# The last layer norm: only the mean goes through TensorE's offset product, and the offset row is added by VectorE and GpSimd

## The chip, the cores and the metric

One core of a Trainium2 chip runs the whole kernel. It has five engines that run their own instruction streams and wait for each other by semaphores: TensorE (PE: matrix products into PSUM), VectorE (DVE), ScalarE (ACT), GpSimd (POOL) and SyncE (SP), which here only issues transfers. The metric is device time in microseconds (us): the median of several runs. The profiled execution is one further run, with its own time and its own span from the first to the last instruction.

## The reference: what is computed

Two layers over 256 rows of 2048 columns. Each layer projects the rows, mixes them in three groups of heads, gates, projects back (`out`), adds the residual and normalises:

```python
def layer_norm(x, g, b):
    mu = jnp.mean(xf, axis=-1, keepdims=True)
    var = jnp.mean(jnp.square(xf - mu), axis=-1, keepdims=True)
    y = (xf - mu) * lax.rsqrt(var + LN_EPS) * g + b
...
    out = y @ w_out
    return layer_norm(DEEPNORM_ALPHA * x + out, ln_g, ln_b)
```

The change concerns the norm of the second, last layer alone. With `rstd` for the reciprocal root, the result in each row is `(x - mu) * rstd * g + b`.

## The kernel before

All products are float32 made of three products of split operands, `hi*hi + lo*hi + hi*lo`, accumulated in PSUM over 16 slices of 128. The weights come in by SP's queue, are split by ScalarE and VectorE (`parts`, L126 to L129) and multiplied by the helper `mm` (L102). TensorE works through the groups of columns one after the other.

The 2048 columns of the output projection are four groups of 512 (`columns(n)`, n = 0 to 3), and the 256 rows are two halves (t = 0 and 1). `res` holds residual plus output. Groups 0 to 2 are finished first; `add_residual` adds them to `res`, takes their statistics, and for t = 1 VectorE multiplies them by the gain `g` at once (L1016). The last group (3) is made for t = 0 first, then for t = 1, and the latter ends with its columns 256 to 511 in a bank of their own (`rest`), so that most of the statistics are taken while TensorE still works.

`norm_last` (L704) is that end. For t = 0 everything is done by VectorE while TensorE makes the products of t = 1. For t = 1 the end of the kernel hangs on it, and it goes in two ways:

- Group 3, in two halves of 256 columns, by VectorE: `centred` (L720) computes `(r - mean) * g`, `result` (L750) computes `r * rstd + b` and stores.
- Groups 0 to 2, which hold `x * g` already, by TensorE and then one scaling. The product of the identity and `res` (L767) puts `x * g` into a PSUM bank, exact, in float32. Then `offsets` (L741) adds a product of 8 rows to it: `nparts`, the transposed small table `nt` with the two parts of `-mean` and of the standard deviation `std` for every row of t = 1, times `rows`, the parts of `g` and `b`. The bank then holds `(x - mean) * g + std * b`, and a multiplication by `rstd` out of PSUM (L782 on VectorE, L784 on ScalarE) gives the result, since `std * rstd` is 1.

`scales` (L722) makes `mvt` (mean and variance), `rstd` by a root on ScalarE and a correction step on VectorE, and for t = 1 the table `nt` (mean at L729 and L730, deviation at L736 to L738). Its argument `meanwhile` is work put between the root's start and its use. The table is turned by TensorE (L773) and copied out of PSUM by ScalarE (L774).

TensorE, SP and GpSimd run in the order of the program. VectorE and ScalarE are ordered by a planner that simulates the time, except in the block of `norm_last` from L753 on, where they too keep the program's order. `store` (L744) issues a transfer from SP's queue, or, for the last one (group 2), from ScalarE's. A transfer at the head of a queue that waits for its data holds those behind it. GpSimd does nothing in this tail.

Of the kernel before, what the change touches and what calls it, by code (L numbers as in the profile page):

```python
# [8 lines left out]
F32 = mybir.dt.float32  # L9
# [3 lines left out]
AF = mybir.ActivationFunctionType  # L13
ALU = mybir.AluOpType
# [4 lines left out]
P = 128  # L19
# [17 lines left out]
def hybrid_trunk_kernel(  # L37
# [7 lines left out]
    pe, dve, act, pool, sp = nc.tensor, nc.vector, nc.scalar, nc.gpsimd, nc.sync  # L45
# [51 lines left out]
    def nm(s):  # L97
        uid[0] += 1
        return f"{s}_{uid[0]}"

    def mm(o, l, r, start, stop):
        pe.matmul(o, l, r, start=start, stop=stop, skip_group_check=True)  # L102

    def bank():
        return psa.tile([P, 512], F32, name=nm("bk"), tag="bk")
# [4 lines left out]
    def small(shape, tag, bufs=1):  # L110
        return sm.tile(shape, F32, name=nm(tag), tag=tag, bufs=bufs)

    ident = cst.tile([P, P], F32, name="ident")
# [533 lines left out]
    def columns(n):  # L647
        return slice(n * 512, (n + 1) * 512)
# [7 lines left out]
    def add_residual(n, t, acc, stats, halves=2):  # L656

        r = res[:, t, columns(n)]
        dve.scalar_tensor_tensor(r, r, ALPHA, acc, op0=ALU.mult, op1=ALU.add)  # L659
        for i in range(halves):  # L660
            dve.bn_stats(stats[:, t, 2 * n + i], r[:, i * 256:(i + 1) * 256])
# [42 lines left out]
    def norm_last(accs, rest, stats, gb, rows, more):  # L704

        n = WO_N - 1
        mvt, rstd = [], []  # L710
        nparts = hd.tile([P, P], F32R, name="nparts", tag="qe")
        nt = sm.tile([P, 2, 4], F32R, name="nt1", tag="nt1")
        std = small([P, 1], "std")
        for t in range(2):
            mvt.append(small([P, 2], f"mvt{t}"))
            rstd.append(small([P, 1], f"rstd{t}"))

        def centred(i, t, c0=0, c1=512):
            r = res[:, t, i * 512 + c0:i * 512 + c1]
            dve.scalar_tensor_tensor(r, r, mvt[t][:, 0:1], gb[i][0][:, c0:c1], op0=ALU.subtract, op1=ALU.mult)  # L720

        def scales(t, meanwhile):  # L722
            dve.bn_aggr(mvt[t], stats[:, t])  # L723
            u, v = small([P, 1], f"rs_u{t}"), small([P, 1], f"rs_v{t}")
            act.activation(u, mvt[t][:, 1:2], AF.Sqrt, bias=eps[:, 0:1])
            dve.tensor_scalar(v, mvt[t][:, 1:2], LN_EPS, -0.5, op0=ALU.add, op1=ALU.mult)
            if t == 1:
                mean = mvt[t][:, 0:1].to_broadcast([P, 2])
                dve.tensor_scalar(nt[:, 0, 0:4:2], mean, -1.0, None, op0=ALU.mult)  # L729
                dve.scalar_tensor_tensor(nt[:, 1, 0:4:2], mean, -1.0, nt[:, 0, 0:4:2].bitcast(F32), op0=ALU.mult, op1=ALU.subtract)  # L730
            meanwhile()
            dve.reciprocal(rstd[t], u)
            dve.scalar_tensor_tensor(u, rstd[t], v, rstd[t], op0=ALU.mult, op1=ALU.mult)
            dve.scalar_tensor_tensor(rstd[t], u, 1.5, rstd[t], op0=ALU.add, op1=ALU.mult)
            if t == 1:
                dve.scalar_tensor_tensor(std, v, -2.0, rstd[t], op0=ALU.mult, op1=ALU.mult)  # L736
                dve.tensor_copy(nt[:, 0, 1:4:2], std.to_broadcast([P, 2]))
                dve.tensor_tensor(nt[:, 1, 1:4:2], std.to_broadcast([P, 2]), nt[:, 0, 1:4:2].bitcast(F32), op=ALU.subtract)  # L738

        def offsets(i, o):  # L740
            mm(o, nparts[:8], rows[i // 2][:8, i % 2 * 512:i % 2 * 512 + 512], False, True)  # L741

        def store(t, cs, queue=sp):
            queue.dma_start(out[t * P:(t + 1) * P, cs], res[:, t, cs])  # L744

        def result(i, t, c0=0, c1=512):

            cs = slice(i * 512 + c0, i * 512 + c1)
            r = res[:, t, cs]
            dve.scalar_tensor_tensor(r, r, rstd[t], gb[i][1][:, c0:c1], op0=ALU.mult, op1=ALU.add)  # L750
            store(t, cs)

        with tc.manual_schedule(engines={DVE, mybir.EngineType.Activation}):  # L753

            add_residual(n, 0, accs[0], stats)
            scales(0, lambda: centred(n, 0))
            result(n, 0)
            for i in range(n):
                centred(i, 0)
                result(i, 0)  # L760
            with tc.high_priority(AHEAD):
                more(0)
                add_residual(n, 1, accs[1], stats, 1)
                more(1)
                o = [psd.tile([P, 2, 512], F32, name=nm("acc"), tag="acc")[:, 0], bank(), bank()]
                for i in (1, 2, 0):
                    mm(o[i], ident, res[:, 1, columns(i)], True, False)  # L767
                r = res[:, 1, n * 512 + 256:n * 512 + 512]
                dve.tensor_tensor(r, r, rest, op=ALU.add)  # L769
                dve.bn_stats(stats[:, 1, 2 * n + 1], r)  # L770
                scales(1, lambda: centred(n, 1, 0, 256))
                pt = bank()
                pe.transpose(pt[:8, :P], nt.rearrange("p a b -> p (a b)").bitcast(F32), ident)  # L773
                act.copy(nparts[:8], pt[:8, :P])  # L774
                result(n, 1, 0, 256)
                centred(n, 1, 256, 512)
                result(n, 1, 256, 512)
                for i in (1, 0, 2):
                    offsets(i, o[i])
                    r = res[:, 1, columns(i)]  # L780
                    if i == 0:
                        dve.tensor_scalar(r, o[i], rstd[1], None, op0=ALU.mult)  # L782
                    else:
                        act.activation(r, o[i], AF.Copy, scale=rstd[1])  # L784
                    store(1, columns(i), act if i == 2 else sp)


    zeros = hd.tile([P, P], F32, name="zeros", tag="st")
# [5 lines left out]
    res = per.tile([P, 2, D], F32, name="res")  # L794
# [3 lines left out]
    for l in range(L):  # L798
# [90 lines left out]
        bias = {}  # L889
# [67 lines left out]
        last = l == L - 1  # L957
        stats = small([P, 2, 2 * WO_N, 6], "stats")
        gb = []
# [8 lines left out]
        for n in range(WO_N):  # L968
# [4 lines left out]
            if last and n == WO_N - 1:  # L973


                accs = [psd.tile([P, 2, 512], F32, name=nm("acc"), tag="acc")[:, 0], bank()]
                rest = bank()[:, :256]
                both = [operand()[2].rearrange("p (h k) n -> p h k n", h=2),
                        per.tile([P, 2, 2, 512], F32R, name=nm("late"), tag="asv")]
                homes = {pc: (x[:, 0], x[:, 1]) for pc, x in zip((2, 3), both)}  # L980
                for i, pc in enumerate((4, 5)):
                    homes[pc] = [per.tile([P, 2, 512], F32R, name=nm("late"), tag=f"yr{2 * i + k}") for k in range(2)]
                ws = [piece(src[pc], 512, 2, homes.get(pc)) for pc in range(8)]

                def products(o, t, kts, cs=slice(0, 512), first=0):
                    for kt in kts:
                        as_products(o, t, yq, [w[:, :, cs] for w in ws[kt // 2]], kt, kt % 2, first)

                products(accs[0], 0, range(16))

                def more(i):
                    if i == 0:
                        products(accs[1], 1, range(12))
                        products(accs[1][:, :256], 1, range(12, 16), slice(0, 256))
                    else:
                        products(rest, 1, range(12, 16), slice(256, 512), 12)

                norm_last(accs, rest, stats, gb, rows, more)
                break
# [4 lines left out]
            for m, pc in order:  # L1004
# [6 lines left out]
                if pc == 7:  # L1011
                    for t in range(2):
                        add_residual(m, t, accs[m][:, t], stats)
                    if last:
                        r = res[:, 1, columns(m)]
# [94 lines left out]
```

## Time and profile before

| | us |
|---|---|
| median of 3 runs | 900.3 |
| lowest and highest run | 900.08, 900.83 |
| the profiled execution, own time | 900.78 |
| its span | 899.0 |
| TensorE busy in the span | 891.3 |
| VectorE busy | 611.8 |
| ScalarE busy | 478.6 |
| GpSimd busy | 214.4 |

In the rows of the profile, a line of the timeline has start, duration, engine, source line, operation, what is written and read, and the count; in brackets the engine's idle time before it and what ended that wait. A name ending in q is an engine's queue, where transfers are issued. `bk` and `acc` are PSUM banks, `sc` are buffers that here hold `g` and `b` of a group, `gbrow` is a buffer of `rows`. A float32 product of 128x512 shows as two matrix instructions. A row of the transfers gives the count, the size of each and the time from issue to landing; a row by stretch gives the busy time of each engine with the count of its instructions.

### The profile page before, as it was taken

To read this page: it belongs to the slowest core of one execution; us is meant where nothing else is said; L and a number is where in the kernel's file an instruction comes from. 1 tells how busy PE (TensorE), PEld (TensorE's weight loads), DVE (VectorE), ACT (ScalarE), POOL (GpSimd) and SP (SyncE) were. 2 spreads that over 40 slices of the span, in tenths; PEclk is the share of its full clock that TensorE was granted. 3 is DMA by queue.
4 is the path that set the end of the run, shared out by engine and by line. 5 is a ranking of instruction groups with operands and counts; after the bars stand their busy time and mean duration, and the time that the engine had idled before them with its cause. 6 is when DMAs were issued, how large, how long until landed. Compare 5 with 4: busy or idle time off the path is not lost.

```text
span 899.0 us, 13806 instructions
## 1 busy us (share of the span) xinstructions
PE 891.3 (99%) x4687; PEld 746.6 (83%) x4687; DVE 611.8 (68%) x887; ACT 478.6 (53%) x686; POOL 214.4 (24%) x401
## 2 busy tenths in 40 slices
PE   9999999999999999999999999999999999999997
PEld 7888988888988888888888888888888888888885
DVE  6756568767477667665587777796565767676766
ACT  6644575555445566544476444854744457565440
POOL 0022103115315443410000221231061344433200
PEclk9999999999999999999999999999999999999999
DMA  8887779867989797975675859697479897979762
GB/s 309 310 260 226 231 235 268 262 207 220 275 254 241 236 271 238 316 236 188 227 241 184 233 164 286 195 292 213 150 224 296 244 270 221 287 217 289 218 183 94
DMA packets 164838, 213.74 MB, mean 238 GB/s; under 512 B 24752, under 2 KB 142896, under 8 KB 164768
## 3 DMA queue, kind: packets, MB, share of 16 engines
q1 hardware_dynamic: 148256, 173.29, 63.4%
q0 software_dynamic: 16224, 39.18, 15.2%
q8 instruction: 37, 0.61, 0.3%
q10 hardware_dynamic: 288, 0.39, 0.1%
q14 instruction: 33, 0.27, 0.1%
HBM read 193.20 MB, written 19.53 MB: 237 GB/s over the span
## 4 chain that ended last, share of the span: by engine, by line
PE 98%; DMA 1%; DVE 0%; ACT 0%; SPq 0%; issue 0%
PE acc L102 91%; PE bk L102 6%; DMA raw<-w 1%; PE bk L626 0%; ACT res L784 0%; SPq L179 0%; ACT wh L128 0%; DVE stats L770 0%; DVE res L769 0%; SPq L203 0%; SPq L201 0%; DVE res L720 0%; DVE mvt L723 0%; PE bk L773 0%; ACT nparts L774 0%
## 5 line engine op out<-in xcount | busy, mean ns | idle before, releaser
L102 PE MATMUL acc<-wh,x 128*128 128x512 f32 (+2 forms) x2516 | 749.4, 381 | 0.4 <-ACT wh L128 0.2
L102 PEld LDWEIGHTS acc<-wh,x 128*128 128x128 f32 x2516 | 460.7, 188 | 87.0 <-ACT wh L128 1.3
L129 DVE TENSOR_TENSOR wl<-raw,wh 128x1024 fp32r<-128x1024 f32 (+3 forms) x321 | 368.2, 1151 | 209.5 <-ACT wh L128 204.9
L128 ACT CAST wh<-raw 128x1024 fp32r<-128x1024 f32 (+3 forms) x321 | 318.7, 996 | 346.6 <-PE acc L102 212.8
L102 PE MATMUL acc<-wl,x 128*128 128x512 f32 (+2 forms) x1258 | 476.6, 379 | 0.0
L102 PEld LDWEIGHTS acc<-wl,x 128*128 128x128 f32 x1258 | 236.2, 188 | 45.6 <-DVE wl L129 1.1
L527 POOL DMA_DIRECT2D home<-sc x70 | 39.2, 560 | 458.1 <-DVE sc L525 442.6
L532 POOL DMA_DIRECT2D pT<-home x96 | 52.5, 553 | 28.5 <-DMA home<-sc 12.8
L532 POOL DMA_DIRECT2D qk<-home x64 | 34.9, 553 | 30.4 <-DMA home<-sc 28.5
L532 POOL DMA_DIRECT2D zT<-home x48 | 26.2, 552 | 21.8 <-DMA home<-sc 14.0
L525 DVE STREAM_TRANSPOSE sc<-sc 128x512 f32<-128x512 f32 (+1 forms) x38 | 24.9, 667 | 3.7 <-ACT sc L950 3.0
L532 POOL DMA_DIRECT2D yr<-home x48 | 26.3, 555 | 3.2 <-DMA home<-sc 3.2
L525 DVE STREAM_TRANSPOSE sc<-acc 128x512 f32<-128x512 f32 x28 | 18.3, 691 | 5.0 <-PE acc L102 4.8
L554 ACT ACTIVATE sc<-sc,mx 128x128 f32<-128x128 f32 (+1 forms) x32 | 14.4, 449 | 13.0 <-DVE mx L552 13.0
L547 DVE SCALAR_TENSOR_TENSOR sc<-bk,bias 128x384 f32<-128x384 f32 x16 | 8.6, 538 | 10.7 <-PE bk L102 10.7
L128 ACT CAST x<-sc 128x512 fp32r<-128x512 f32 x20 | 12.3, 617 | 5.0 <-DVE sc L508 3.8
L129 DVE TENSOR_TENSOR x<-sc,x 128x512 fp32r<-128x512 f32 x20 | 13.7, 685 | 1.4 <-ACT x L128 1.4
L102 PEld LDWEIGHTS bk<-pT,asv 128*128 128x128 f32 x64 | 11.8, 189 | 1.8
L102 PE MATMUL bk<-qk,qk 128*128 128x128 f32 (+1 forms) x64 | 13.1, 326 | 0.0
L102 PE MATMUL bk<-pT,asv 128*128 128x256 f32 (+1 forms) x64 | 13.0, 326 | 0.0
L659 DVE SCALAR_TENSOR_TENSOR res<-res,acc 128x512 f32<-128x512 f32 x15 | 9.7, 681 | 4.0 <-PE acc L102 4.0
L129 DVE TENSOR_TENSOR x<-raw,x 128x1024 fp32r<-128x1024 f32 x5 | 6.1, 1226 | 8.9 <-ACT x L128 8.8
(204 smaller groups left out, 506.4 us busy)
## 6 DMA issues: line engine op xcount, KB each, us to landing
raw<-w SPq DMA_DIRECT2D x387, 256.0 KB, 4.7
raw<-w SPq DMA_DIRECT2D x62, 512.0 KB, 4.9
home<-sc POOLq DMA_DIRECT2D x54, 256.0 KB, 4.3
raw<-w SPq DMA_DIRECT2D x32, 388.0 KB, 5.1
raw<-w SPq DMA_DIRECT2D x32, 264.0 KB, 3.3
qk<-home POOLq DMA_DIRECT2D x64, 64.0 KB, 5.2
raw<-w SPq DMA_DIRECT2D x32, 124.0 KB, 4.8
bias<-relw SPq DMA_DIRECT2D x16, 192.0 KB, 4.6
```

What stands on the lines that cost most here:

```text
L102: pe.matmul(o, l, r, start=start, stop=stop, skip_group_check=True)
L128: keep(act.copy(hi, src))
L129: keep(dve.tensor_tensor(lo, src, hi.bitcast(F32), op=ALU.subtract))
L525: dve.transpose(blocks.rearrange(order, j=32), src.rearrange("p (g b j) -> p g b j", b=4, j=32))
L527: pool.dma_start(homes[-1], blocks)
L532: pool.dma_start(dst[b * 32:(b + 1) * 32], home[:, b].rearrange("(a i) n -> i a n", a=4))
L547: dve.scalar_tensor_tensor(s, pb[:, :384], SCALE, bias[h], op0=ALU.mult, op1=ALU.add)
L554: act.activation(s[:, own[t]], s[:, own[t]], AF.Exp, bias=mx[:, t:t + 1], accum_out=zs[:, t:t + 1])
L659: dve.scalar_tensor_tensor(r, r, ALPHA, acc, op0=ALU.mult, op1=ALU.add)
```

## The change

The deviation no longer goes through the offset product. Its two places in `nt` are set to zero once, ahead of the block, and the three instructions that made it (L736 to L738) are gone; the bank then holds `(x - mean) * g`, and `b` is added behind the scaling by `rstd`.

- TensorE's order: the identity products of groups 2 and 0, the turning of `nt`, the offsets of groups 2 and 0, then the identity product and the offset of group 1. The turning and the copy `nparts` now stand inside `meanwhile`.
- Groups 0 and 1: VectorE computes `o * rstd + b` from PSUM in one instruction each.
- Group 2: ScalarE scales from PSUM, GpSimd adds `b` (512 columns).
- The second half of group 3 leaves VectorE: ScalarE computes `mean - r`, GpSimd multiplies by `g` (256 columns), ScalarE scales, and GpSimd subtracts from `b` (256 columns).
- The stores of both halves of group 3, of group 0 and of group 2 are on SP's queue, in this order; that of group 1 is on ScalarE's queue, behind its other work.

```diff
-        std = small([P, 1], "std")
+        dve.memset(nt.bitcast(F32), 0.0)
...
-            if t == 1:
-                dve.scalar_tensor_tensor(std, v, -2.0, rstd[t], op0=ALU.mult, op1=ALU.mult)
-                dve.tensor_copy(nt[:, 0, 1:4:2], std.to_broadcast([P, 2]))
-                dve.tensor_tensor(nt[:, 1, 1:4:2], std.to_broadcast([P, 2]), nt[:, 0, 1:4:2].bitcast(F32), op=ALU.subtract)
...
-                for i in (1, 2, 0):
+                for i in (2, 0):
                     mm(o[i], ident, res[:, 1, columns(i)], True, False)
                 r = res[:, 1, n * 512 + 256:n * 512 + 512]
                 dve.tensor_tensor(r, r, rest, op=ALU.add)
                 dve.bn_stats(stats[:, 1, 2 * n + 1], r)
-                scales(1, lambda: centred(n, 1, 0, 256))
-                pt = bank()
-                pe.transpose(pt[:8, :P], nt.rearrange("p a b -> p (a b)").bitcast(F32), ident)
-                act.copy(nparts[:8], pt[:8, :P])
+
+                def meanwhile():
+                    centred(n, 1, 0, 256)
+                    act.activation(r, r, AF.Identity, bias=mvt[1][:, 0:1], scale=-1.0)
+                    pool.tensor_tensor(r, r, gb[n][0][:, 256:], op=ALU.mult)
+                    pt = bank()
+                    pe.transpose(pt[:8, :P], nt.rearrange("p a b -> p (a b)").bitcast(F32), ident)
+                    act.copy(nparts[:8], pt[:8, :P])
+                    for i in (2, 0):
+                        offsets(i, o[i])
+                    mm(o[1], ident, res[:, 1, columns(1)], True, False)
+                    offsets(1, o[1])
+
+                scales(1, meanwhile)
                 result(n, 1, 0, 256)
-                centred(n, 1, 256, 512)
-                result(n, 1, 256, 512)
-                for i in (1, 0, 2):
-                    offsets(i, o[i])
-                    r = res[:, 1, columns(i)]
+                act.activation(r, r, AF.Copy, scale=rstd[1])
+                pool.tensor_tensor(r, gb[n][1][:, 256:], r, op=ALU.subtract)
+                store(1, slice(n * 512 + 256, n * 512 + 512))
+                last = res[:, 1, columns(2)]
+                act.activation(last, o[2], AF.Copy, scale=rstd[1])
+                pool.tensor_tensor(last, last, gb[2][1], op=ALU.add)
+                for i in (0, 1):
+                    dve.scalar_tensor_tensor(res[:, 1, columns(i)], o[i], rstd[1], gb[i][1], op0=ALU.mult, op1=ALU.add)
                     if i == 0:
-                        dve.tensor_scalar(r, o[i], rstd[1], None, op0=ALU.mult)
-                    else:
-                        act.activation(r, o[i], AF.Copy, scale=rstd[1])
-                    store(1, columns(i), act if i == 2 else sp)
+                        store(1, columns(0))
+                        store(1, columns(2))
+                store(1, columns(1), act)
```

## The prediction

> **What bounds the kernel now.** I read the page first: its busy times, its DMA slices and the chain that ended last.
>
> ```profile
> span 899.0 us, 13806 instructions
> PE 891.3 (99%) x4687; PEld 746.6 (83%) x4687; DVE 611.8 (68%) x887; ACT 478.6 (53%) x686; POOL 214.4 (24%) x401
> ...
> PE 98%; DMA 1%; DVE 0%; ACT 0%; SPq 0%; issue 0%
> ```
>
> TensorE carries the span; the change touches no product of the layers. What is left to win or lose is the tail, where TensorE has no more products and the second half of the rows (128 rows, "t = 1") gets its norm. The timeline of the last 12 us shows it (start, duration, engine, line, what it writes and reads):
>
> ```profile
> 887.52 0.69 DVE L659 SCALAR_TENSOR_TENSOR res<-res,bk 128x512 f32<-128x512 f32 x1 [1.25 <-PE bk L102]
> 888.76 1.88 PE L102 MATMUL bk<-res,ident 128*128 128x512 f32 x4
> ...
> 890.28 0.29 ACT L725 ACTIVATE rs_u<-mvt,eps 128x1 f32<-128x1 f32 x1 [10.19 <-DVE mvt L723]
> 890.48 1.02 PE L102 MATMUL acc<-res,ident 128*128 128x512 f32 x2
> 890.54 0.16 DVE L730 SCALAR_TENSOR_TENSOR nt<-mvt,nt 128x2 fp32r<-128x2 f32 x1
> 890.62 0.48 DVE L720 SCALAR_TENSOR_TENSOR res<-res,mvt,sc 128x256 f32<-128x256 f32 x1
> ...
> 891.46 0.16 DVE L734 SCALAR_TENSOR_TENSOR rstd<-rs_u,rstd 128x1 f32<-128x1 f32 x1
> 891.65 0.16 DVE L736 SCALAR_TENSOR_TENSOR std<-rs_v,rstd 128x1 f32<-128x1 f32 x1
> 891.85 0.17 DVE L737 CAST nt<-std 128x2 fp32r<-128x2 f32 x1
> 892.05 0.16 DVE L738 TENSOR_TENSOR nt<-std,nt 128x2 fp32r<-128x2 f32 x1
> 892.13 0.48 DVE L750 SCALAR_TENSOR_TENSOR res<-res,rstd,sc 128x256 f32<-128x256 f32 x1
> 892.36 0.27 PE L773 MATMUL bk<-ident,nt 128*8 128x128 f32 x1 [0.86 <-DVE nt L738]
> 892.53 0.48 DVE L720 SCALAR_TENSOR_TENSOR res<-res,mvt,sc 128x256 f32<-128x256 f32 x1
> 892.67 0.25 ACT L774 CAST nparts<-bk 8x128 fp32r<-8x128 f32 x1 [2.09 <-PE bk L773]
> 892.97 0.49 PE L102 MATMUL bk<-gbrow,nparts 8*128 8x512 f32 x1 [0.34 <-ACT nparts L774]
> 893.04 0.48 DVE L750 SCALAR_TENSOR_TENSOR res<-res,rstd,sc 128x256 f32<-128x256 f32 x1
> 893.31 0.39 PE L102 MATMUL acc<-gbrow,nparts 8*128 8x512 f32 x1
> 893.50 1.26 ACT L784 ACTIVATE res<-bk,rstd 128x512 f32<-128x512 f32 x2 [0.58 <-PE bk L102]
> 893.54 0.39 PE L102 MATMUL bk<-gbrow,nparts 8*128 8x512 f32 x1
> 893.74 0.75 DVE L782 TENSOR_SCALAR res<-acc,rstd 128x512 f32<-128x512 f32 x1 [0.22 <-PE acc L102]
> ```
>
> The offset product needs the mean and the standard deviation. The mean's two parts are ready at 890.70 (L730); TensorE's transposition waits for the deviation's until 892.21 (L738). Behind it stand the copy (L774), the offset products and the scaling of groups 1, 0 and 2 out of PSUM. The last scaling ends at 893.50 + 1.26 = 894.76. Then come the stores; first their issues in the timeline, then their landing times, then the busy times by stretch (last columns: clock, DMA share, GB/s):
>
> ```profile
> 892.63 0.33 SPq L744 DMA_DIRECT2D out<-res  x1
> 893.55 0.33 SPq L744 DMA_DIRECT2D out<-res  x1
> 894.22 0.81 SPq L744 DMA_DIRECT2D out<-res  x2
> 894.80 0.35 ACTq L744 DMA_DIRECT2D out<-res  x1
> ```
>
> ```profile
> out<-res SPq DMA_DIRECT2D x6, 256.0 KB, 2.4
> out<-res SPq DMA_DIRECT2D x2, 128.0 KB, 1.9
> out<-res ACTq DMA_DIRECT2D x1, 256.0 KB, 3.2
> ```
>
> ```profile
> 894.00:895.00 1.00, 0.00 (x0) 0.00 (x0) 0.49 (x1) 0.77 (x2) 0.00 (x0) 1.00 0.37 131
> 895.00:896.00 1.00, 0.00 (x0) 0.00 (x0) 0.00 (x0) 0.00 (x0) 0.00 (x0) 1.00 0.95 356
> 896.00:897.00 1.00, 0.00 (x0) 0.00 (x0) 0.00 (x0) 0.00 (x0) 0.00 (x0) 0.51 1.02 375
> 897.00:899.00 2.00, 0.00 (x0) 0.00 (x0) 0.00 (x0) 0.00 (x0) 0.00 (x0) 0.50 0.08 28
> ```
>
> The last store lands at 894.80 + 3.2 = 898.0, and 1.0 us of closing follows to 899.0. Three 256 KB stores issued within 0.6 us share the DMA engines at some 375 GB/s, which is why the last takes 3.2 and not 2.4.
>
> **The change, part by part.** All times are on this execution's clock. Its own time is 900.78, which is 0.48 above the median of the runs (900.3); I add my difference to the median. Waits between engines cost 0.04 (L773 ends at 892.63, L774 starts at 892.67), and 0.15 from VectorE to TensorE (892.21 to 892.36).
>
> *Removed from VectorE:* L736 to L738, from 891.65 to the start of L750 at 892.13, 0.48 on the path; the second half of group 3 (the L720 at 892.53 and the L750 at 893.04), which goes to ScalarE and GpSimd. *Added:* a memset of 8 columns, bounded by 0 and by the 0.16 of a small VectorE operation; it depends on nothing and is covered by VectorE's idle 1.25 in front of L659. Without that cover it costs those 0.16. I take 0.
>
> *TensorE.* Six passes of the three ident products (two each) run from 888.76 at (890.48 − 888.76) / 4 = 0.43 a pass. Now only groups 2 and 0 come first, four passes, so TensorE is free at 890.48 and the transposition starts when the mean is there: 890.70 + 0.15 = 890.85, to 891.12. The copy runs from 891.16 to 891.41, behind the new Identity on ScalarE (below, to 891.05, so it isn't held). Offset products start at 891.46: group 2 is done 0.49 later, at 891.95; group 0 starts 0.34 after, at 891.80, done at 892.19. Then two passes for group 1 from 892.03 (0.23 after, as 893.31 to 893.54), and its offset from 892.89 to 893.28. Group 1 was the first to be finished and is now the last. If the transposition waited for something else, all three would move by as much.
>
> *VectorE.* L750 for the first half starts at 891.65 and ends at 892.13 (0.48 earlier); its store is issued at 892.17. The two final operations replace a scaling (L782, 0.75) by scaling and addition in one. The trace has no such operation with PSUM and SBUF and a scalar; L659 (0.69, same inputs, constant scalar) and L782 (0.75, scalar per row) bound it, and I take 0.75 for the scalar. Group 0: 892.23 to 892.98. Group 1: waits for TensorE to 893.32, ends at 894.07; ScalarE's queue issues its store at 894.11.
>
> *ScalarE and GpSimd.* These rows (line, shapes, count, busy, mean ns) are the nearest prices:
>
> ```profile
> L554 ACT ACTIVATE sc<-sc,mx 128x256 f32<-128x256 f32 x16 | 7.9, 496 | 0.0
> L784 ACT ACTIVATE res<-bk,rstd 128x512 f32<-128x512 f32 x2 | 1.3, 683 | 0.6 <-PE bk L102 0.6
> ```
>
> ```profile
> L353 POOL MEMSET sc<- 128x512 f32 x2 | 1.1, 526 | 0.1
> L299 POOL MEMSET gw<- 128x256 f32 x2 | 0.7, 332 | 0.0
> ```
>
> Identity on 256 columns (0.50, L554) follows L725 (ends 890.57): to 891.05. GpSimd has done no arithmetic on two inputs in this kernel. The memset bounds it from below, 0.33 for 256 columns and 0.53 for 512; from above I take three memsets, one for each stream read or written: 1.00 and 1.58. I take two, 0.66 and 1.05, since the two reads may overlap the write. So: multiplication m from 891.10 to 891.76; ScalarE's scaling (0.50; the scale was ready at 891.62) 891.80 to 892.30; subtraction s 892.34 to 893.00; its store is at the head of SP's queue at 893.04 (893.55 before), and that of group 0, ready since 892.98, queues behind it until 893.37. ScalarE scales group 2 from 892.30 to 892.98 (0.68); GpSimd's addition a runs 893.04 to 894.09; its store, now on SP, goes at 894.13. In short, that issue is at 891.76 + (m + s + a), with 2.37 in the bracket. Nothing waits behind it on SP.
>
> *The shared port.* L750 on VectorE (two SBUF inputs) runs 891.65 to 892.13 beside GpSimd's m to 891.76: 0.11 of overlap in my schedule. No row here has two such instructions at once; the bounds are 0 and the whole 0.48, and I take 0. The final VectorE operations read PSUM and one SBUF input. The Trainium skill ("GPSIMD Engine Reference", section 1, Specifications) says that GpSimd shares its SBUF interfaces with VectorE and contends with VectorE instructions that have two SBUF inputs. By that, m would end later by up to L750's length and the sum would fall from 0.67 to 0.19; no run here shows it yet.
>
> *The sum.* The last issue goes from 894.80 to 894.13 (SP) and 894.11 (ScalarE): 0.67 earlier, two ends almost together. Of the three 256 KB stores, group 0's leaves about 0.7 ahead of the other two. Their landing lies between 2.4 and 3.2; two stores at 375 GB/s still take 1.4 us of transfers, so I keep 3.2 and give back 0.07 for two queues at once: 0.6 gained. Prediction: 900.3 − 0.6 = 899.7 (a span of 898.4). A difference of 0.2% is 1.8 us, about what a measurement of this kernel can tell from no change; 0.6 is a third of it.
>
> **Rivals.**
> *GpSimd becomes the bound (slower).* At the upper prices the bracket is 1.00 + 1.00 + 1.58 = 3.58, the last store is issued at 895.34, 0.54 later than before: 900.8. It decides from m + s + a = 3.04 on (the old 894.80), that is 2.6 memsets per operation; a loss over 0.2% needs 4.84. For it: three steps in a row cross between GpSimd and ScalarE. Against: all three would have to take 2.6 times a memset of their size, and ScalarE, which alternates with GpSimd, has no other work between these steps.
>
> *GpSimd pays once for its first arithmetic instruction.* Nothing in the trace shows it: GpSimd's rows are memsets and DMA issues. The one-off that the trace shows elsewhere is ScalarE's table load:
>
> ```profile
> 873.34 1.28 ACT L725 ACT_TABLE_LOAD   x1
> ```
>
> With 1.28 ahead of m, the last issue would be at 895.41: 900.9. The Trainium skill ("GPSIMD Engine Reference", section 2.1, Instruction dispatch) puts the first call of a freshly loaded GpSimd kernel at about 6 us; an estimate from that page's figure is 900.3 + 5.3 = 905.6, if this operation counts as freshly loaded.
>
> *The transfers hide the gain.* If the bytes of the four stores and not their issue set the end, half of it is lost: 900.0. For it: 375 GB/s through 895 to 897. Against: at 894 to 895 only 131 GB/s.
>
> *The stores part.* If the last two land in 2.4 as the undisturbed ones do, the gain is 0.67 + 0.8 = 1.5: 898.8.
>
> **How the numbers follow.** Likeliest, 0.50: 899.7, its own range 899.2 to 900.3. GpSimd the bound 0.23 (900.8), transfers 0.12 (900.0), stores part 0.10 (898.8), first-use cost 0.05 (900.9 and above). The runs before spread from 900.08 to 900.83, which widens every case by 0.4. The range goes from 898.8 to 901.0: it leaves out some of the first-use case and the upper part of a slow GpSimd. Faster by over 0.2% only at the far end of the parted stores: 0.03. Slower by over 0.2%: 0.05 from GpSimd and 0.03 from the first-use case, 0.08. Within: 0.89.
>
> **What would show it.** The transposition starts near 890.85 and waits for the mean's parts; TensorE ends with group 1's offset near 893.3. GpSimd shows three instructions: their lengths, and whether the first is longer than the second (both 256 columns), tell the slow case from the first-use case. The last VectorE operation ends near 894.1 and is released by TensorE. The last SP store is issued near 894.1. The prediction fails if m + s + a exceeds 3.0, if the transposition waits for ScalarE or memory, or if VectorE's and ScalarE's work ahead of 887 is ordered anew and TensorE stalls there.

## The result, and the profile after

| | before | after |
|---|---|---|
| median of 8 runs, us | 900.37 | 903.38 |
| lowest and highest | 900.04, 901.99 | 902.78, 903.94 |
| the profiled execution, own time | 900.78 | 902.87 |
| its span | 899.0 | 900.7 |

The ratio after / before is 1.0029, 95% interval 1.002 to 1.0039: slower by 3.0 us, where 0.6 faster was forecast. The order of the tail's own work nevertheless came out as drawn; only its last parts came later, GpSimd's end by 0.5 us. The timeline of the changed kernel, in parts (start, duration, engine, line, what is written and read):

```profile
887.32 0.69 DVE L659 SCALAR_TENSOR_TENSOR res<-res,bk 128x512 f32<-128x512 f32 x1 [1.25 <-PE bk L102]
890.08 0.29 ACT L725 ACTIVATE rs_u<-mvt,eps 128x1 f32<-128x1 f32 x1 [10.19 <-DVE mvt L723]
890.28 0.49 ACT L770 ACTIVATE res<-res,mvt 128x256 f32<-128x256 f32 x1
890.56 0.27 PE L773 MATMUL bk<-ident,nt 128*8 128x128 f32 x1
890.85 0.72 POOL L771 TENSOR_TENSOR res<-res,sc 128x256 f32<-128x256 f32 x1 [41.28 <-ACT res L770]
891.01 0.58 DVE L733 SCALAR_TENSOR_TENSOR rs_u<-rstd,rs_v 128x1 f32<-128x1 f32 x1
891.88 0.51 ACT L782 ACTIVATE res<-res,rstd 128x256 f32<-128x256 f32 x1 [0.75 <-DVE rstd L734]
892.46 0.72 POOL L783 TENSOR_TENSOR res<-sc,res 128x256 f32<-128x256 f32 x1 [0.89 <-ACT res L782]
893.15 1.26 POOL L787 TENSOR_TENSOR res<-res,sc 128x512 f32<-128x512 f32 x1
893.43 0.75 DVE L789 SCALAR_TENSOR_TENSOR res<-bk,rstd,sc 128x512 f32<-128x512 f32 x1 [0.46 <-PE bk L102]
893.64 1.13 SPq L740 DMA_DIRECT2D out<-res  x2
894.21 0.35 ACTq L740 DMA_DIRECT2D out<-res  x1
```

The tail starts 0.2 earlier than in the profile of before (L659 at 887.32 against 887.52). The last VectorE operation ends at 894.18, GpSimd's addition at 893.15 + 1.26 = 894.41; the last store issue starts near 894.4, against 894.80 before. The busy times by stretch show the transfers (the last column is GB/s):

```profile
895.00:896.00 1.00, 0.00 (x0) 0.00 (x0) 0.00 (x0) 0.00 (x0) 0.00 (x0) 0.50 1.01 381
896.00:897.00 1.00, 0.00 (x0) 0.00 (x0) 0.00 (x0) 0.00 (x0) 0.00 (x0) 0.50 0.65 234
897.00:898.00 1.00, 0.00 (x0) 0.00 (x0) 0.00 (x0) 0.00 (x0) 0.00 (x0) 0.50 0.00 0
898.00:899.00 1.00, 0.00 (x0) 0.00 (x0) 0.00 (x0) 0.00 (x0) 0.00 (x0) 0.50 0.00 0
```

All bytes are out before 897; before the change some 56 KB were still moving after 897. Then no engine and no transfer is busy for almost four microseconds. What lasts is in the instructions that close the program, which the page of the profile doesn't count as busy. All of them stand on one line of the kernel. This is, in part, the view of that closing line in the kernel before (queue, operation, count, duration in ns min/median/max, first and last start in us):

```profile
L1106 POOLq DRAIN  x3: 46/98/9174, 848.8 to 898.7; - x3
L1106 SPq DRAIN  x3: 7/7/7, 898.2 to 898.5; - x3
```

and the same in the changed kernel:

```profile
L1114 POOLq EVENT_SEMAPHORE  x4: 17/17/17, 899.9 to 900.6; - x4
L1114 POOLq DRAIN  x3: 46/98/6890, 893.0 to 900.4; - x3
L1114 SPq DRAIN  x3: 7/7/7, 897.7 to 900.2; - x3
L1114 DVEq DRAIN  x2: 19/404/789, 893.4 to 900.2; - x2
L1114 ACTq DRAIN  x2: 8/80/153, 894.6 to 900.2; - x2
```

SP's first closing instruction starts at 897.7 instead of 898.2: SP is through with the stores 0.5 us earlier, of which 0.2 is the earlier start of the tail and 0.3 the gain of the change. But GpSimd's queue holds an instruction called DRAIN that takes 6.89 us. It begins at 893.0, before GpSimd's last addition has started, and ends at 899.89, 5.5 us behind the end of that addition. The last drains of the other queues start only behind it, at 900.2, and 0.8 us after its end the span ends. Before, the drain was even longer, 9.17 us, but it began at 848.8, behind GpSimd's last transfer, and was over at 858.0, 40 us before anyone needed it.

Since executions reach the tail at different times (the root, ScalarE's operation at L725, starts between 889.78 and 891.41 in the runs below), "tail" here means the time from that start to the end of the span. Before: 899.0 − 890.28 = 8.72. After: 900.7 − 890.08 = 10.62, so 1.90 longer. The two profiled executions differ by 2.09 in their own time: 1.90 in the tail, less 0.20 for the earlier root, and 0.39 outside the span. The latter isn't chance of one run: in its eight runs, the changed kernel's time is 2.06 to 2.19 above its span; in the five kernels e1 to e5 below and the runs of before beside them it is 1.73 to 1.92. The remaining 0.9 of the 3.0 is how far the two profiled executions lie from their medians (the changed one 0.51 below, the one of before 0.41 above); no trace shows where those other executions spent it. Neither this nor the part outside the span has been traced to a cause.

### The profile page after: what moved, and what is told of

Read it like the earlier page. It is cut to its first block, busy times and chain, and to the rows that moved or that the text cites. A ratio compares the mean times of both kernels' runs of the same rounds, so it can differ in the third digit from the quotient of the medians.

```text
span 900.7 us, 13810 instructions
## 1 busy us (share of the span) xinstructions
PE 891.6 (99%) x4687; PEld 747.1 (83%) x4687; DVE 611.5 (68%) x884; ACT 478.7 (53%) x687; POOL 217.2 (24%) x404
## 4 chain that ended last, share of the span: by engine, by line
PE 96%; DMA 1%; issue 1%; DVE 1%; ACT 0%; POOLq 0%; POOL 0%; SPq 0%; DVEq 0%; ACTq 0%
PE acc L102 89%; PE bk L102 6%; DMA raw<-w 1%; PE bk L626 0%; DVE wl L129 0%; POOLq L1114 0%; POOL res L771 0%; DVE sc L366 0%; DVE res L659 0%; ACT qk L924 0%; ACT sc L365 0%; DVE yr L366 0%; DVE qe L381 0%; SPq L153 0%; ACT sc L364 0%
## 5 line engine op out<-in xcount | busy, mean ns | idle before, releaser
L659 DVE SCALAR_TENSOR_TENSOR res<-res,acc 128x512 f32<-128x512 f32 x15 | 9.6, 681 | 5.1 <-PE acc L102 5.1
L532 POOL DMA_DIRECT2D yT<-home x16 | 8.7, 550 | 15.3 <-DMA home<-sc 15.3
```

The costliest lines, as they stand in the source:

```text
L532: pool.dma_start(dst[b * 32:(b + 1) * 32], home[:, b].rearrange("(a i) n -> i a n", a=4))
```

## The experiments

**What sets the end.** Four kernels, e1 to e4, tell the closing drain (theory D) from a first-use cost of GpSimd's arithmetic (F) and from the new order of the stores (S); a fifth, e5, looks for the place from which the drain does no harm.

*e1: the three operations on VectorE.*

```diff
-                    pool.tensor_tensor(r, r, gb[n][0][:, 256:], op=ALU.mult)
+                    dve.tensor_tensor(r, r, gb[n][0][:, 256:], op=ALU.mult)
...
-                pool.tensor_tensor(r, gb[n][1][:, 256:], r, op=ALU.subtract)
+                dve.tensor_tensor(r, gb[n][1][:, 256:], r, op=ALU.subtract)
...
-                pool.tensor_tensor(last, last, gb[2][1], op=ALU.add)
...
                         store(1, columns(0))
+                        dve.tensor_tensor(last, last, gb[2][1], op=ALU.add)
                         store(1, columns(2))
```

> The changed kernel with its three GpSimd operations given to VectorE, nothing else. Theory D (closing drain): in the changed kernel GpSimd's drain at the program's end lasts until 899.89, 5.5 us behind GpSimd's last instruction (894.41), and the close waits for it; without GpSimd work in the tail the drain lies back at 849 as before and is covered. Then the end is set by the stores again: VectorE has 0.42 + 0.42 + 0.68 us more to do, its last operation ends near 895.2, the last store lands near 898.2: time 900.6 (900.0 to 901.2). Rival F (a first-use cost of GpSimd arithmetic): the same here. Rival S (the new order of the stores makes them land late): the order is kept, so 903 or more.

Measured: 899.77 against 900.59, ratio 0.9991 (0.9981 to 1.0); tail 8.22. The median is below the expected range. VectorE's last operation ends at 894.37, not 895.2: counted from the root, it ends only 0.49 later than in the changed kernel, although VectorE has 1.52 more to do. Its wait for TensorE ahead of the last operation (0.46) is filled, and L733 is 0.36 shorter (below). The drain is back at its old place:

```profile
L1114 POOLq DRAIN  x3: 46/98/9686, 848.3 to 897.7; - x3
L1114 SPq DRAIN  x3: 7/7/7, 897.2 to 897.5; - x3
```

S falls: with the stores in the same order, the time is back. As soon as GpSimd is out of the tail, the tail is 0.50 shorter than before. That the median (899.77) meets the forecast (899.7) is in part luck: the kernel before measured 900.59 beside it and not 900.3, and the gain has another source than the one forecast. The last store is issued no earlier, at 4.63 behind the root against 4.52 before:

```profile
894.41 0.35 ACTq L740 DMA_DIRECT2D out<-res  x1
```

It lands 2.6 later in place of 3.2. The stores ahead of it had started earlier: from 3 to 4 and from 4 to 5 us behind the root 261 and 304 GB/s move, where the kernel before had 131 and 215.

*e2: the kernel before, with one late memset on GpSimd, a piece of 8x128.*

```diff
                     store(1, columns(i), act if i == 2 else sp)
+                pool.memset(nparts[:8].bitcast(F32), 0.0)
```

> The kernel before, and one GpSimd memset of 8x128 behind the last offset product (which ends at 893.93 in the kernel before). Theory D: the memset ends near 894.1, the drain 5.5 us later at 899.6, the close 0.8 after that: span 900.4, time 901.8 (+1.5). Rival F (arithmetic on GpSimd costs, a memset doesn't): 900.3, no change. Rival S: 900.3.

Measured: 901.92 against 900.59, ratio 1.0016 (1.0007 to 1.0026); tail 901.1 − 890.91 = 10.19, 1.47 longer than before.

```profile
894.69 0.20 POOL L786 MEMSET nparts<- 8x128 f32 x1 [44.27 <-PE bk L102]
...
L1107 POOLq DRAIN  x3: 46/98/5690, 894.7 to 900.9; - x3
L1107 SPq DRAIN  x3: 7/7/7, 898.8 to 900.6; - x3
```

Two tenths of a microsecond of work, on an engine with nothing else to do and nobody waiting for its result, cost 1.3 in the median and 1.47 in the tail: its drain ends at 900.4, SP was ready at 898.8. F falls: no arithmetic is needed.

*e3: the same kind of instruction (128x2 elements), but some 8.5 us earlier.*

```diff
                 result(i, 0)
+            pool.memset(mvt[0], 0.0)
```

> The kernel before, and one GpSimd memset of 128x2 behind the results of the first half of the rows (about 886.3). Theory D: the drain runs from about 886.4 to 892 and is covered by the rest: 900.3, no change. A rival by which any GpSimd instruction behind its last transfer lengthens the end, wherever it stands: +1 or more.

Measured: 900.68 against 900.59, ratio 1.0002 (0.9992 to 1.0011); tail 8.75.

```profile
885.98 0.10 POOL L761 MEMSET mvt<- 128x2 f32 x1 [35.82 <-DVE res L720]
...
L1107 POOLq DRAIN  x3: 46/98/5595, 886.0 to 899.1; - x3
```

Again 5.5 us behind the instruction, from 886.1 to 891.6, and free. In this kernel the place of GpSimd's last instruction counts, not that there is one.

*e4: only the last addition on VectorE; multiplication and subtraction stay on GpSimd.*

```diff
-                pool.tensor_tensor(last, last, gb[2][1], op=ALU.add)
...
                         store(1, columns(0))
+                        dve.tensor_tensor(last, last, gb[2][1], op=ALU.add)
                         store(1, columns(2))
```

> The changed kernel with only the last addition (group 2) moved from GpSimd to VectorE; multiplication and subtraction stay on GpSimd, so its last instruction ends at 893.2 instead of 894.41. Theory D: the drain ends 1.2 earlier, at 898.7, and still sets the end: 902.2 (901.7 to 902.6). Rival F: the first arithmetic instruction is still there, 903.4. Rival S: the stores go as before, 903.4.

Measured: 901.09 against 900.59, ratio 1.0005 (0.9995 to 1.0015); tail 899.2 − 889.78 = 9.42, 1.20 shorter than the changed kernel's, as forecast from GpSimd's end.

```profile
892.17 0.73 POOL L783 TENSOR_TENSOR res<-sc,res 128x256 f32<-128x256 f32 x1 [0.89 <-ACT res L782]
...
L1114 POOLq DRAIN  x3: 46/98/6247, 892.1 to 898.9; - x3
```

The drain ends at 898.4, 5.5 behind the subtraction (892.90). The time missed the expected range, 901.09 instead of 902.2: it fell by 2.3, not by 1.2. Of the 1.9 by which the two profiled executions differ, 1.2 is the tail, 0.3 an earlier root and 0.4 the part outside the span; the rest of the 2.3 isn't explained.

*e5: only the multiplication left on GpSimd; the addition moved as in e4, and the subtraction too.*

```diff
-                pool.tensor_tensor(r, gb[n][1][:, 256:], r, op=ALU.subtract)
+                dve.tensor_tensor(r, gb[n][1][:, 256:], r, op=ALU.subtract)
```

> The changed kernel with only the multiplication by the gain left on GpSimd; subtraction and addition on VectorE. The multiplication ends near 891.3. Theory D: the drain ends 5.5 later, near 896.8, before the last store lands (897.3), so it is covered and the end is as with all three on VectorE: 899.7 (899.3 to 900.2). The rival that the drain's tail depends on the kind or number of GpSimd instructions: anything from 900.3 to 901.1. The short VectorE operation at L733 again takes 0.58 instead of 0.22 beside the multiplication, if the two share a port.

Measured: 900.49 against 900.63, ratio 0.9999 (0.9991 to 1.0008); tail 8.29, as e1's 8.22. The multiplication ends at 892.91, the drain at 898.4, SP is ready at 898.9: covered, by half a microsecond. The median itself missed the range: this kernel's runs fall into a lower and an upper group (899.7 to 900.5, and 901.1 to 901.9). The profiled one (901.49) is in the upper, with the root 1.1 later than in the kernel before; so its surplus is ahead of the tail, and the cause is open.

**A tail without GpSimd that keeps the deviation in the offset product** (w1, w2). The deviation comes from ScalarE's root itself. ScalarE scales groups 2 and 0 and one half of group 1, VectorE does group 3 and the other half of group 1. In part, w1 against the kernel before:

```diff
+                dve.tensor_copy(nt[:, 0, 1:4:2], u.to_broadcast([P, 2]))
+                dve.tensor_tensor(nt[:, 1, 1:4:2], u.to_broadcast([P, 2]), nt[:, 0, 1:4:2].bitcast(F32), op=ALU.subtract)
             meanwhile()
...
-            if t == 1:
-                dve.scalar_tensor_tensor(std, v, -2.0, rstd[t], op0=ALU.mult, op1=ALU.mult)
...
+                dve.tensor_scalar(res[:, 1, cs], o[1][:, :256], rstd[1], None, op0=ALU.mult)
...
+                act.activation(res[:, 1, cs], o[1][:, 256:], AF.Copy, scale=rstd[1])
```

w2 differs from w1 in TensorE's order:

```diff
-                for i in (2, 0):
+                for i in (2, 0, 1):
                     mm(o[i], ident, res[:, 1, columns(i)], True, False)
...
-                    for i in (2, 0):
+                    for i in (2, 0, 1):
                         offsets(i, o[i])
-                    mm(o[1], ident, res[:, 1, columns(1)], True, False)
-                    offsets(1, o[1])
```

> No GpSimd in the tail, and the deviation stays in the offset product, but is taken from ScalarE's root itself (no longer from the corrected reciprocal), so it is there 1.2 us earlier, beside the mean. TensorE's order as in the changed kernel (group 1 last). ScalarE scales groups 2 and 0 and half of group 1, VectorE does group 3 and the other half of group 1. Worked out from the rows: offset table copied near 891.8, offsets done 892.4 to 893.7, last scaling near 894.0 on the clock of the kernel before, against 894.76: 899.5 (899.1 to 900.0), as fast as with all three operations on VectorE or 0.3 faster.

> The same with the three identity products ahead of the transposition, as in the kernel before, so all three offsets follow each other. The transposition starts 0.3 later, group 1 is ready 0.6 earlier: 899.4 (899.0 to 900.0).

Measured: w1 899.91, ratio 0.9992 (0.9983 to 1.0001), tail 7.89; w2 899.98, ratio 0.9992 (0.9983 to 1.0001), tail 8.17. They are 0.4 and 0.6 above what was worked out, inside the ranges. The two halves of group 1 did not run side by side: the row of ScalarE's half in w1 names VectorE's half as what it waited for, though they write other columns (they read the same bank). In w2 ScalarE's half starts behind VectorE's, too; why isn't shown.

```profile
893.82 0.48 DVE L788 TENSOR_SCALAR res<-bk,rstd 128x256 f32<-128x256 f32 x1 [0.56 <-PE bk L102]
894.34 0.47 ACT L791 ACTIVATE res<-bk,rstd 128x256 f32<-128x256 f32 x1 [0.97 <-DVE res L788]
```

With e1 these are the fastest here, 0.65 to 0.82 below the kernel before, at the edge of what the runs can tell from no change.

**Why the drain takes 5.5 us.** Small programs, which leave out the whole computation of the reference: VectorE does some 29 us of work, and GpSimd then one addition of 128x512. Each was run once. The first three differ in who issues one load and who does the addition (`pool` or `sp` for the load, `pool` or `dve` for the addition):

```diff
+    pool.dma_start(g, ln_g[0:1, 0:512].to_broadcast([P, 512]))
...
+    for _ in range(40):
+        dve.tensor_tensor(h, h, g, op=ALU.mult)
+    pool.tensor_tensor(h, h, g, op=ALU.add)
```

> A small program that leaves out the whole computation: it copies the input to the output, VectorE does 41 operations in a row (some 28 us), and one GpSimd addition of 128x512 waits for the last of them. GpSimd issues no transfer. If the drain's 5.5 us belong to GpSimd's last instruction as such, it is 5.5 again and the program ends about 6.3 us behind that addition. If they belong to the transfers that GpSimd issued before, the drain is short, under 1 us.

> The same, but one of the loads (128x512) is issued by GpSimd at the start. If the drain belongs to the last instruction: 5.5, as without. If it belongs to issued transfers: some us longer than without.

> The same without a GpSimd operation behind VectorE's chain (the addition is VectorE's). The drain stands at the start and is covered: the program ends about 1 us behind VectorE's last operation, some 5 us earlier than with the GpSimd addition.

Measured: 42.13, 42.06 and 41.56. The drain is short, also behind one transfer, and taking the addition off GpSimd saves 0.6 and not 5. First the rows without a GpSimd transfer, then the drain with one:

```profile
38.36 1.26 POOL L56 TENSOR_TENSOR h<-h,g 128x512 f32<-128x512 f32 x1 [37.92 <-DVEq L140]
L140 POOLq DRAIN  x3: 34/70/1364, 38.3 to 40.1; - x3
```

```profile
L140 POOLq DRAIN  x3: 34/78/1458, 38.1 to 40.0; - x3
```

It lasts 0.1 and 0.2 longer than the addition. So the 5.5 us do not belong to GpSimd's last instruction as such. The next six add what the large kernel's GpSimd has most of, transfers (386 of its 401 instructions), or as many memsets. N is the count. One further operation, not shown here, makes VectorE's work wait for the last of them:

```diff
+    for i in range(384 - N, 384):
+        pool.dma_start(many[:, i], ln_g[0:1, 0:8].to_broadcast([P, 8]))
```

> The small program (no computation of the reference) with 96 transfers issued by GpSimd at the start, then VectorE's chain and GpSimd's one addition. The drain ended 0.04 us behind that addition without a transfer and 0.14 with one, against 5.5 in the large kernel, in which GpSimd issues some 380 transfers. If the drain's tail grows with the number of transfers that GpSimd has issued: about 1.4. If it grows with the number of GpSimd's instructions, much the same, 1.4. If it is something else of the large kernel: under 0.3.

> The same with 384 transfers. By number of transfers: about 5.5. By something else of the large kernel: under 0.3.

> The same with 384 GpSimd memsets of 128x8 in place of the transfers. By number of transfers: under 0.1. By number of instructions: about 5.5. By something else: under 0.3.

> The small program (no computation of the reference) with 8 transfers issued by GpSimd. A step at few transfers: 5 to 8 us behind the addition. Growth with the count: near 0.7. A saw-tooth with a period over 100: near 0.7, too.

> The same with 32 transfers. A step: 5 to 8. Growth or a saw-tooth: about 2.6, a third of the 7.9 with 96.

> The same with 192 transfers. A step: 5 to 8, as with 96 and 384. Growth up to a limit: between 7.9 and 5.5, no longer. A saw-tooth: anything, under 3 or over 8 among them.

Measured, the row of the drain in each (8, 32, 96, 192 and 384 transfers, one kernel a fence), and last 384 memsets:

```profile
L144 POOLq DRAIN  x3: 34/95/2037, 47.5 to 50.0; - x3
```

```profile
L144 POOLq DRAIN  x3: 34/95/3997, 77.8 to 82.3; - x3
```

```profile
L144 POOLq DRAIN  x3: 40/95/9231, 154.8 to 164.5; - x3
```

```profile
L144 POOLq DRAIN  x3: 40/95/8412, 270.2 to 279.1; - x3
```

```profile
L144 POOLq DRAIN  x3: 40/95/6781, 501.7 to 508.9; - x3
```

```profile
L144 POOLq DRAIN  x3: 34/70/1364, 44.2 to 45.9; - x3
```

Beyond the addition's 1.26 the drain lasts 0.8, 2.7, 8.0, 7.2, 5.5 and 0.1 us. Transfers make it, instructions don't. Up to 96 it grows by (7.97 − 0.10) / 96 = 0.082 us for each transfer, so that 96 cost 8.0 where 1.4 had been expected; with 192 and 384 it is shorter again, as if 106 transfers were taken off once and three times. With 384 it is 5.5, as in the large kernel with its 386. The 7.2 with 192 also lies where growth up to a limit had been expected (between 7.9 and 5.5), so 106 is no more than a guess from two points. It was then put to the large kernel.

**The count in the large kernel.** The changed kernel with tiny transfers added at its start, 850 us ahead of the tail, where GpSimd is idle:

```diff
     dve.memset(eps[:, 1:2], RMS_EPS)
+    spare = ident[0:1, :88]
+    for i in range(44):
+        pool.dma_start(spare[:, 2 * i:2 * i + 2], ln_g[0:1, 2 * i:2 * i + 2])
```

> The changed kernel with 44 GpSimd transfers of 8 bytes added at its start, where GpSimd is idle; nothing else is changed, the three operations in the tail stay on GpSimd. If the drain's length is 0.082 us for each transfer beyond the last multiple of 106: 386 + 44 = 430 leaves 6, the drain ends 0.5 us behind the addition, at 894.9, long before the last store lands, and the end is set by the stores: 899.7 (899.2 to 900.3), faster than the kernel before, as predicted for the change at first. If the 5.5 us are a fixed price of the large kernel: 903.4 or more.

> The changed kernel with 20 such transfers added. By the count: 406 leaves 88, the drain ends 7.2 us behind the addition instead of 5.5: 905.1 (904.7 to 905.5). If the price is fixed: 903.4.

Measured: with 44, 905.24 against 900.53, ratio 1.0052 (1.004 to 1.0065); with 20, 902.73, ratio 1.0025 (1.0016 to 1.0034). The count failed in both. A fixed price failed, too: with 20 the time is below its 903.4, and the drains below are not 5.5. With 44:

```profile
893.72 1.26 POOL L787 TENSOR_TENSOR res<-res,sc 128x512 f32<-128x512 f32 x1
...
L1117 POOLq DRAIN  x3: 46/98/9098, 893.6 to 903.2; - x3
```

with 20:

```profile
893.00 1.26 POOL L787 TENSOR_TENSOR res<-res,sc 128x512 f32<-128x512 f32 x1
...
L1117 POOLq DRAIN  x3: 46/98/7298, 892.9 to 900.7; - x3
```

The drain ends 7.7 and 5.9 us behind the addition, against 5.5 without added transfers. With the roots at 890.65 and 889.93 the tails are 12.85 and 11.07, 2.2 and 0.45 longer than the changed kernel's 10.62. So transfers issued at the very start, and long landed, do lengthen the drain at the end. From 20 to 44 it grows by 1.8 / 24 = 0.075 for each, near the 0.082 of the small programs; but the first 20 brought 0.45 and not 1.6, and the wrap at multiples of 106 isn't there. By what rule it falls back stays open. The median with 20 lies 0.65 below the changed kernel's although its tail is longer; the changed kernel's 0.3 outside the span is absent here (1.73 to 1.89, as elsewhere), and the rest isn't explained.

## Why the prediction was wrong, point by point

*The removal and TensorE's order: right.* The transposition was put at 890.85; it started at 890.56, and 0.2 of that is the earlier tail. Group 1's offset product, put to end at 893.28 (893.08 on this clock), ends at 893.39, 0.3 late, and VectorE follows at 893.43.

*GpSimd's operations: right within the bounds.* m, s and a took 0.72, 0.72 and 1.26, a sum of 2.70 against the 2.37 taken, and below the 3.04 from which GpSimd was to decide. So that rival, which carried most of the case of slower, did not happen in the form given. The first operation is as long as the second and starts 0.08 behind the Identity that it waits for (890.77): there is no first-use cost. The Trainium skill ("GPSIMD Engine Reference", section 2.1, Instruction dispatch) gives about 6 us for the first call of a freshly loaded kernel. No wait of that kind is in this trace, so the page's rule isn't contradicted; the operation just shows no such load.

*The shared port: a cost I had put at nothing, in another place.* L750 was the operation I had watched; in the changed kernel (there L746, from 891.82) it runs between two GpSimd operations and meets neither. It was L733, one element a row with two SBUF inputs, that stood still: 0.58 beside the multiplication, and its end (891.59) is the multiplication's (891.57). In e1, without GpSimd, it takes 0.22:

```profile
891.04 0.22 DVE L733 SCALAR_TENSOR_TENSOR rs_u<-rstd,rs_v 128x1 f32<-128x1 f32 x1
```

e4 and e5, which keep the multiplication on GpSimd, show 0.59 again. The price is 0.36 on the way to `rstd`; it made ScalarE's scaling (L782) and with it s start some 0.3 later than forecast. The Trainium skill's sentence on the shared interfaces ("GPSIMD Engine Reference", section 1, Specifications), told in the prediction, agrees with these rows.

*The stores: right in direction, half in size.* The last issue was to come 0.67 earlier. Counted from the root it came 0.16 earlier (4.36 against 4.52): of the missing 0.5, 0.3 is L733's, and 0.2 is a, 1.26 in place of 1.05. Counted so, SP is through 0.3 earlier; 0.6 was forecast. And it isn't the last issue alone that sets when the stores are through: e1 issues its last store 0.11 later than the kernel before and is through 0.5 earlier; its bytes had begun to move sooner. The sum had no term for this; the rival "the transfers hide the gain" was nearer to it.

*The closing: the step that failed.* "The last store lands at 894.80 + 3.2 = 898.0, and 1.0 us of closing follows to 899.0": I carried the close over as a constant behind the last store. It is a meeting of all engines, and each queue brings its own drain. GpSimd's, 9.17 us, stood in the profile of before; I passed over it because GpSimd had no busy instruction after 849 and the drain isn't one. It had been over 40 us before anyone needed it. The change put GpSimd's last instruction 1.9 us behind the latest place that would have kept the old end: SP ready at 898.2, less 5.5, is 892.7, which is 2.4 behind the root; GpSimd's addition ended 4.3 behind it. The sum had asked of GpSimd only when its results were needed, not when the engine could be let go. With the stores alone setting the end (e1) the tail is 0.5 shorter than before; with the drain it is 1.9 longer. The other 1.1 of the 3.0 has no cause shown.

## What to carry to other kernels

Before giving an engine its last instruction in a kernel's tail, look at the closing line's drains of that engine, which are in no busy time, and ask where the drain would end from the new place. Here, in kernels whose GpSimd issues some 400 transfers, GpSimd's last instruction had to end 5.5 us before SP was through with the last store; the multiplication alone was covered (e5), subtraction and addition were not. With other numbers of transfers the 5.5 is another number, and no rule for it was found. Comparing tails from a common event (here the root) rather than whole times took out the differences ahead of the tail (the root alone varies by 1.6 us among the runs above), and made effects of half a microsecond visible.

## What the runs showed of the hardware

- GpSimd's drain at the program's end lasted until 5.5 us behind its last instruction in the large kernel (386 transfers), whether that was a memset of 8x128, one of 128x2, a multiplication or a subtraction of 128x256, or an addition of 128x512. In small programs this was 0.1 without GpSimd transfers, also after 384 memsets, and 0.8, 2.7 and 8.0 with 8, 32 and 96 transfers, the last of which had landed some 30 us before. With 192 and 384 it was 7.2 and 5.5, and in the large kernel with 20 and 44 more transfers 5.9 and 7.7.
- GpSimd's two-input float32 operation took 0.72 for 256 columns and 1.26 for 512, about 2.1 ns a column and 0.18 besides.
- A VectorE operation of one element a row, with two inputs in SBUF, lasted until the end of a GpSimd multiplication beside it: 0.58 in place of 0.22. VectorE's last operation, with one input in PSUM and one in SBUF, took 0.75 beside GpSimd's addition and 0.74 without it (e1).
